# Context squares kept out of PSUM, the residual's gate row moved beside the heads of x, and another share of PSUM for the output units

## The chip, the cores and the metric

The kernel runs on one core of one Trainium2 chip. The metric is the device time of one execution in microseconds (us). TensorE is the engine PE of the profile, VectorE is DVE, ScalarE is ACT, GpSimd is POOL, SyncE is SP; SP computes nothing here and issues most DMAs.

## What is computed

One layer of a hybrid backbone on 1024 latent tokens (`x`) and 256 context tokens (`ctx`), width 2048, all in fp32. Cut to what matters:

```
mod = silu(c) @ w_mod + b_mod           # shift, scale and gate rows; ctx uses c_ctx
h   = rmsnorm(x) * (1 + scale) + shift  # the same for ctx with its own row
q,k,v,o,z,gates,xr,zr = split(h @ w_in) # x and ctx share the weights
A = mlstm(q, k, v, gates) * sigmoid(o) * silu(z)       # 4 heads, both directions, state from ctx
B = rglru(conv(xr)) * silu(zr)                         # 8 tiles of 128 channels, both directions
out = rmsnorm(x + gate * (concat(A, B) @ w_out)) * final_g
```

The change concerns the norm of ctx (the mean of its squares over 2048 channels), the row `gate` of `mod` (2048 numbers), the softplus of the RG-LRU's `lambda`, and the accumulators of the last matmul.

## The kernel before

Every fp32 product is made of three fp32r products: a weight tile `raw` comes by DMA on SP (`Ring._dma`, L206), ACT rounds it to `whi` (L227), DVE takes the rest `wlo = raw - whi` (L228), and PE multiplies hi by hi, hi by lo and lo by hi. The class `Ring` does this ahead of use, with two or three pieces in hand.

The work runs in five stages. **Phase A** (to about 169 us of the span) squares x, multiplies the modulation weights `wm` with silu(c) and silu(c_ctx) (`mv_group`, L471), turns x into normalised tiles `hxh`/`hxl` (`to_hx`, L536 to L542), and beside that accumulates the first three column tiles of `h @ w_in` (`main_a`, L595). In it the context norm is computed: at the end of iterations j = 2 and 3, `ctx_norms` squares four pairs of ctx tiles in one go (L559) into PSUM tiles `mx`, and DVE adds them up (L561, L563); `ctx_pair` then makes `hch`/`hcl` (L577 to L581), one tile k after the other through a single buffer `ft`. The order on PE, DVE, ACT and SP in phase A is the order of the code (`in_order`). **The context heads** (to about 360 us) begin with V of ctx (`cv`, L976 to L978); ahead of it stand the evacuation of phase A's three accumulators (L659 to L669) and the softplus chain of lambda (L674 on). **The heads of x** (to about 1167 us) interleave column tiles (L1200 to L1206), V (L1243 to L1246) and the mLSTM scans (`scan_gen`, L1131 on; its decay rows `NI` come by DMA on SP, L1079). The context's RG-LRU, `ctx_rg_all`, runs beside them in slots `RS` of 128x260. **The rg stage** (to about 1533 us) computes column tiles xr and zr and, beside them, the RG-LRU of x (`rg_gen`: L689 conv, L904 to L906 scan, L920; L1308 to L1320 gates), and also the residual's gate row (`gt_gen`, L1329 to L1350): 64 weight tiles `gw` of 128x512 come by DMA through two buffers, DVE multiplies and adds each into `ga` (L1336, L1338), four matmuls with ones sum over the partitions (L1344), and a DMA stores the row. **The output units** (to the end) multiply with `w_out` (L1425 to L1427), eight units of 512 tokens by 512 columns.

After phase A the order comes from a planner: `Clock` holds the side work as generators, each of which yields an estimated time, and takes the next step of each when the main work's `tick` has advanced that far. PSUM has two tiles `mm` of two banks and four tiles `mx` of one bank. An output unit needs four banks:

```
if db % 2:
    return [mx_tile() for _ in range(4)]
two = [mm_tile() for _ in range(2)]
```

A `ct_unit` of the rg stage also uses `mm`, and L1407/L1408 evacuate it.

Of the kernel before, what the change touches and what calls it, by code (L numbers as in the profile page):

```python
# [150 lines left out]
class Ring:  # L151


    def __init__(self, tc, pool, nraw, npc, raw_el, pc_el):
# [10 lines left out]
        self.pri = 0  # L165

# [47 lines left out]
    def _split(self):  # L214
# [33 lines left out]
def tile_hymba(ctx: ExitStack, tc: tile.TileContext, x, x_t, ctx_t, vecs_t, w_mod_a, w_mod_g, b_mod, w_in,  # L248
# [182 lines left out]
    def load_ctx(j):  # L431
        for k in (2 * j, 2 * j + 1):
            Xc[k] = hcs.tile([128, CTX], F32, tag="cl", bufs=KT, name=f"cT{k}")
            SP.dma_start(out=Xc[k], in_=ctx_t[k])

    def phase_a():
        ACT.dma_start(out=cols, in_=vecs_t[:, 0:216])
        cc = pa.tile([128, 4, 16], F32, tag="ft", bufs=1, name="cc")
# [15 lines left out]
        del cc  # L454
        DVE.tensor_scalar(out=b1sc, in0=cols[:, cSC:cSC + 16], scalar1=1.0, scalar2=None, op0=ADD)
# [99 lines left out]
        def ctx_norms(js):  # L555
# [43 lines left out]
        ctx_at = {4: (0, 1), 5: (2, 3), 6: (4, 5), 7: (6, 7)}  # L599
        for j in range(KP):  # L600
            for u in range(2):
# [972 lines left out]
```

## Time and profile before

| | us |
|---|---|
| median of 3 runs (1921.99 to 1927.17) | 1925.8 |
| the profiled execution | 1922.13 |
| its span, first to last instruction | 1920.4 |
| PE busy | 1825.2 (95%) |
| DVE busy | 891.8 (46%) |
| ACT busy | 778.4 (41%) |
| POOL busy | 280.9 (15%) |

The mean granted clock of TensorE was 0.982 of full speed. Busy shares are means over stages; where PE waited must be read stage by stage. In a timeline row the bracket at the end tells how long the engine had been idle before the row and what ended it. In a row of windows the number behind each engine is its busy time and, in parentheses, how many instructions.

### The profile page before, as it was taken

How to read it: one execution, taken by the hardware profiler on the slowest of the kernel's cores; microseconds unless marked ns; L12 is line 12 of the kernel's file. 1: busy time of each engine (PE TensorE's matmuls, PEld its weight loads, DVE VectorE, ACT ScalarE, POOL GpSimd, SP SyncE). 2: the span in 40 equal slices, each digit the busy share in tenths (PEclk: the TensorE clock that was granted, in tenths of full speed). 3: DMA queues.
4: the chain of work that ended last, by engine and by line, in shares of the span. 5: the costliest groups of instructions: out<-in, count | busy, mean ns of one | idle time of the engine just before them, and what ended most of it. 6: DMA issues, size and time to landing. Idle time of an engine off the chain costs nothing.

```text
span 1920.4 us, 23817 instructions
## 1 busy us (share of the span) xinstructions
PE 1825.2 (95%) x9106; PEld 1489.9 (78%) x9106; DVE 891.8 (46%) x1565; ACT 778.4 (41%) x1214; POOL 280.9 (15%) x382
## 2 busy tenths in 40 slices
PE   7888999999999999999999999889899989999997
PEld 2446999888897879887898878667777767887786
DVE  5556653445434542145213435775575555334432
ACT  5335543336735531133113334455555554224322
POOL 0000001012101110011001201221212323222221
PEclk9999999999999999999999999899999989999999
DMA  9965575213222222122121215333342336446533
GB/s 382 337 212 169 166 195 142 78 50 69 64 72 56 52 65 66 45 55 68 55 60 45 66 34 154 109 110 96 89 131 70 105 119 200 129 132 220 167 113 132
DMA packets 217283, 224.48 MB, mean 117 GB/s; under 512 B 24760, under 2 KB 169272, under 8 KB 217168
## 3 DMA queue, kind: packets, MB, share of 16 engines
q1 hardware_dynamic: 209128, 199.16, 35.0%
q10 hardware_dynamic: 5256, 14.88, 2.1%
q0 software_dynamic: 2784, 8.92, 1.4%
q8 instruction: 71, 1.16, 0.2%
q14 instruction: 44, 0.36, 0.1%
HBM read 202.92 MB, written 20.00 MB: 116 GB/s over the span
## 4 chain that ended last, share of the span: by engine, by line
PE 74%; DMA 9%; DVE 8%; issue 4%; ACT 3%; POOL 1%; ACTq 0%; SPq 0%; DVEq 0%; POOLq 0%
PE mm L1206 12%; PE mm L1200 12%; PE mm L1203 12%; PE mm L595 2%; PE mm L1243 2%; PE mm L1245 2%; PE mm L1246 2%; DMA gw<-in_w_mod_g_dram 2%; DMA yst<-yD 2%; PE mx L1426 2%; PE mx L1427 2%; PE mx L1425 2%; PE mm L1425 2%; PE mm L1426 2%; PE mm L1427 2%
## 5 line engine op out<-in xcount | busy, mean ns | idle before, releaser
L228 DVE TENSOR_TENSOR wlo<-raw,whi 128x512 fp32r<-128x512 f32 (+2 forms) x396 | 285.8, 731 | 599.3 <-ACT whi L227 598.4
L227 ACT ACTIVATE whi<-raw 128x512 fp32r<-128x512 f32 (+2 forms) x396 | 243.4, 624 | 603.1 <-PE mm L1203 254.0
L1206 PE MATMUL mm<-hxh,wlo 128*128 128x512 f32 x1184 | 377.2, 400 | 14.2 <-DVE wlo L228 14.1
L1200 PE MATMUL mm<-hxh,whi 128*128 128x512 f32 x1184 | 388.3, 409 | 0.3 <-DVE Gx L1232 0.3
L1203 PE MATMUL mm<-hxl,whi 128*128 128x512 f32 x1184 | 374.4, 397 | 0.0
L1206 PEld LDWEIGHTS mm<-hxh,wlo 128*128 128x128 f32 x1184 | 224.9, 190 | 67.8 <-DVE wlo L228 16.4
L1203 PEld LDWEIGHTS mm<-hxl,whi 128*128 128x128 f32 x1184 | 224.6, 190 | 53.0
L1200 PEld LDWEIGHTS mm<-hxh,whi 128*128 128x128 f32 x1184 | 222.9, 190 | 50.7 <-issue 1.4
L1243 PE MATMUL mm<-whi,hxh 128*128 128x256 f32 x384 | 109.9, 286 | 0.4 <-DVE s L1281 0.2
L1425 PE MATMUL mm<-whi,hxh 128*128 128x512 f32 x256 | 102.7, 402 | 6.4 <-DVE s L1408 6.2
L1245 PE MATMUL mm<-wlo,hxh 128*128 128x256 f32 x384 | 108.2, 282 | 0.0
L1246 PE MATMUL mm<-whi,hxl 128*128 128x256 f32 x384 | 107.6, 281 | 0.0
L1426 PE MATMUL mm<-wlo,hxh 128*128 128x512 f32 x256 | 102.7, 401 | 2.7 <-DVE wlo L228 2.7
L1427 PE MATMUL mm<-whi,hxl 128*128 128x512 f32 x256 | 102.1, 399 | 0.0
L1425 PE MATMUL mx<-whi,hxh 128*128 128x512 f32 x192 | 76.1, 397 | 4.0 <-ACT whi L227 4.0
L1426 PE MATMUL mx<-wlo,hxh 128*128 128x512 f32 x192 | 76.0, 396 | 1.7 <-DVE wlo L228 1.7
L1427 PE MATMUL mx<-whi,hxl 128*128 128x512 f32 x192 | 75.5, 393 | 0.0
L1338 DVE SCALAR_TENSOR_TENSOR ga<-gw,cols,ga 128x512 f32<-128x512 f32 x60 | 55.1, 918 | 43.7 <-DMA gw<-in_w_mod_g_dram 43.2
L1243 PEld LDWEIGHTS mm<-whi,hxh 128*128 128x128 f32 x384 | 72.6, 189 | 1.2 <-issue 0.5
L1245 PEld LDWEIGHTS mm<-wlo,hxh 128*128 128x128 f32 x384 | 72.5, 189 | 0.3
L1246 PEld LDWEIGHTS mm<-whi,hxl 128*128 128x128 f32 x384 | 72.3, 189 | 0.0
L1103 ACT ACTIVATE D<-D,gxAC 128x128 f32<-128x128 f32 x64 | 25.4, 401 | 107.6 <-POOL D L1102 107.4
(320 smaller groups left out, 3092.5 us busy)
## 6 DMA issues: line engine op xcount, KB each, us to landing
raw<-in_w_in_dram SPq DMA_DIRECT2D x134, 512.0 KB, 4.0
wm<-in_w_mod_a_dram SPq DMA_DIRECT2D x64, 512.0 KB, 8.8
raw<-in_w_out_dram SPq DMA_DIRECT2D x64, 512.0 KB, 4.7
gw<-in_w_mod_g_dram SPq DMA_DIRECT2D x64, 256.0 KB, 3.1
xT<-in_x_t_dram SPq DMA_DIRECT2D x16, 512.0 KB, 8.9
NI<-niD SPq DMA_DIRECT2D x64, 128.0 KB, 4.6
xpc<-in_x_dram SPq DMA_DIRECT2D x32, 256.0 KB, 3.4
yD<-s ACTq DMA_DIRECT2D x15, 512.0 KB, 2.9
```

Of the source, the lines that this page charges most:

```text
L227: self.nc.scalar.activation(out=hi, in_=src, func=AF.Copy)
L228: self.nc.vector.tensor_tensor(out=lo, in0=src, in1=hi.bitcast(F32), op=SUB)
L1200: PE.matmul(out=ps[:, ts], lhsT=hi, rhs=hxh[k][:, ts], start=(k == 0), stop=False)
L1203: PE.matmul(out=ps[:, ts], lhsT=hi, rhs=hxl[k][:, ts], start=False, stop=False)
L1206: PE.matmul(out=ps[:, ts], lhsT=lo, rhs=hxh[k][:, ts], start=False, stop=(k == KT - 1))
L1243: PE.matmul(out=o, lhsT=hxh[k][:, sl], rhs=hi, start=(k == 0 and tt % 2 == 0), stop=False, skip_group_check=True)
L1245: PE.matmul(out=o, lhsT=hxh[k][:, sl], rhs=lo, start=False, stop=False, skip_group_check=True)
L1246: PE.matmul(out=o, lhsT=hxl[k][:, sl], rhs=hi, start=False, stop=(k == KT - 1), skip_group_check=True)
L1338: DVE.scalar_tensor_tensor(out=a, in0=t, scalar=silc[:, k:k + 1], in1=a, op0=MUL, op1=ADD)
L1425: PE.matmul(out=pst[jt], lhsT=hxh[j][:, sl], rhs=hi, start=(j == 0), stop=False)
L1426: PE.matmul(out=pst[jt], lhsT=hxh[j][:, sl], rhs=lo, start=False, stop=False)
L1427: PE.matmul(out=pst[jt], lhsT=hxl[j][:, sl], rhs=hi, start=False, stop=(j == KT - 1))
```

## The change

It has seven parts. (1) ctx is loaded in 8 tiles of two k each, and `ctx_norm(j)` squares one such tile in one 512-wide instruction into a half of the SBUF tile `ncp`, one behind each group of modulation matmuls in iterations 2 and 3. (2) `ctx_pair` takes both k of a pair through two halves of `vt`. (3) `Ring` holds back the raw loads of phase A to the beginning of the next iteration. (4) The softplus chain of lambda moves to the beginning of phase A. (5) The first V of ctx is written inside phase A's ordered block, and the evacuation of the accumulators is spread over its k. (6) `gt_gen` goes; `gate_row` follows the context's RG-LRU as a tail of `ctx_rg_all`, in slots `RS`, with 128 tiles of 128x256 and three in flight. (7) Each output unit takes one `mm` tile and two `mx` tiles.

```
+    def release(self):
+        while self.held:
+            self.held -= 1
             self._dma()
...
-            for j in js:
-                sq = mx_tile()
-                for u in range(2):
-                    act(out=sq[:, CTX * u:CTX * u + CTX], in_=Xc[2 * j + u], func=AF.Square)
-                if j == 0:
-                    DVE.tensor_copy(out=ncp[0][:, 0:512], in_=sq)
-                else:
-                    DVE.tensor_tensor(out=ncp[0][:, 0:512], in0=ncp[0][:, 0:512], in1=sq, op=ADD)
+        def ctx_norm(j):
+            sq, sm = ncp[0][:, 512:1024], ncp[0][:, 0:512]
+            act(out=sq if j else sm, in_=Xc[j].rearrange("p u t -> p (u t)"), func=AF.Square)
+            if j:
+                DVE.tensor_tensor(out=sm, in0=sm, in1=sq, op=ADD)
...
+                        if j in (2, 3):
+                            ctx_norm(4 * j - 8 + g)
...
-            if j in (2, 3):
-                ctx_norms(range(4 * j - 8, 4 * j - 4))
...
+        def put_away(k):
+            if k == 4:
+                gate_tile(0)
+            elif k == 6:
+                gate_tile(1)
+            elif k == 8:
+                raw_tile(2, 2)
+        raw_tile(0, 0)
+        ps_v = cv_products(0, put_away)
...
-        xflag["rgctx"] = True
+        yield from gate_row(RS)
+    def gate_row(RS):
+        W = 256
+        todo = [(db, k) for db in range(D // W) for k in range(KT)]
...
+            t = yield from RS.get()
+            SP.dma_start(out=t[:, 0:W], in_=wmod_k[:, k, db * W:(db + 1) * W])
...
+                DVE.scalar_tensor_tensor(out=a, in0=t, scalar=silc[:, k:k + 1], in1=a, op0=MUL, op1=ADD)
+            RS.free()
+            if n + 3 < len(todo):
+                yield from load(n + 3)
+            yield 2.7
+            if k == KT - 1:
+                ps = mx_tile()
+                PE.matmul(out=ps[:, 0:W], lhsT=ones, rhs=a, start=True, stop=True)
...
-    clk.spawn(gt_gen(), 1.0, P['gt'])
...
     def out_tiles(db):
-        if db % 2:
-            return [mx_tile() for _ in range(4)]
-        two = [mm_tile() for _ in range(2)]
-        return [two[j // 2][:, 512 * (j % 2):512 * (j % 2) + 512] for j in range(4)]
+        two = mm_tile()
+        return [two[:, 0:512], two[:, 512:1024], mx_tile(), mx_tile()]
```

How the instructions stand on an engine before and now, at three places. In a row a number behind a name tells buffers of one name apart.

ACT in phase A, iteration 2, before: the squares stand in one block behind the four `hxh`.

```order
L478 ACTIVATE pmS_631<-mx_577 128x512
L537 ACTIVATE hxh_646<-rxt,ssa 128x512 x2
L537 ACTIVATE hxh_654<-rxt,ssa 128x512 x2
L559 ACTIVATE mx_676<-cT_356 128x256
L559 ACTIVATE mx_676<-cT_358 128x256
L559 ACTIVATE mx_680<-cT_360 128x256
L559 ACTIVATE mx_680<-cT_362 128x256
L559 ACTIVATE mx_684<-cT_364 128x256
L559 ACTIVATE mx_684<-cT_366 128x256
L559 ACTIVATE mx_688<-cT_368 128x256
L559 ACTIVATE mx_688<-cT_370 128x256
L227 ACTIVATE whi_692<-raw_517 128x384
```

The same iteration now:

```order
L228 ACTIVATE whi_577<-raw_471 128x384
L591 ACTIVATE ncp<-cT_376 128x512
L591 ACTIVATE ncp<-cT_378 128x512
L591 ACTIVATE ncp<-cT_380 128x512
L228 ACTIVATE whi_625<-raw_471 128x384
L512 ACTIVATE pmS_637<-mx_581 128x512
L591 ACTIVATE ncp<-cT_382 128x512
L571 ACTIVATE hxh_654<-rxt,ssa 128x512 x2
L571 ACTIVATE hxh_662<-rxt,ssa 128x512 x2
L228 ACTIVATE whi_687<-raw_574 128x384
```

Eight squares of one k became four of two k, they write SBUF, and they stand ahead of `hxh`. The line numbers of the changed kernel are its own: its L228, L512, L571 and L591 are L227, L478, L537 and L559 of before.

DVE in the rg stage, around the two scans of one tile, before (L1338 is the gate row, L904 to L906 the scan):

```order
L228 TENSOR_TENSOR wlo_10986<-raw_10703,whi_10985 128x512
L1338 SCALAR_TENSOR_TENSOR ga_10969<-gw_7_11134,cols,ga_10969 128x512
L1338 SCALAR_TENSOR_TENSOR ga_10969<-gw_8_11161,cols,ga_10969 128x512
L904 SCALAR_TENSOR_TENSOR s_10856<-s_10979,s_10856 128x1024
L904 SCALAR_TENSOR_TENSOR s_10911<-s_10982,s_10911 128x1024
L905 TENSOR_TENSOR s_10856<-s_10856,s_10887 128x1024
L905 TENSOR_TENSOR s_10911<-s_10911,s_10943 128x1024
L906 SCALAR_TENSOR_TENSOR s_10887<-s_10979,rini,s_10856 128x1024
L906 SCALAR_TENSOR_TENSOR s_10943<-s_10982,rini,s_10911 128x1024
L228 TENSOR_TENSOR wlo_11030<-raw_10795,whi_11029 128x512
```

And now, where L957 to L959 are that scan:

```order
L229 TENSOR_TENSOR wlo_10967<-raw_10737,whi_10966 128x512
L957 SCALAR_TENSOR_TENSOR s_10847<-s_10960,s_10847 128x1024
L957 SCALAR_TENSOR_TENSOR s_10901<-s_10963,s_10901 128x1024
L958 TENSOR_TENSOR s_10847<-s_10847,s_10877 128x1024
L958 TENSOR_TENSOR s_10901<-s_10901,s_10930 128x1024
L959 SCALAR_TENSOR_TENSOR s_10877<-s_10960,rini,s_10847 128x1024
L959 SCALAR_TENSOR_TENSOR s_10930<-s_10963,rini,s_10901 128x1024
L229 TENSOR_TENSOR wlo_11003<-raw_10737,whi_11002 128x512
```

Nothing stands between the weight split and the scan any more.

DVE beside the scan of head 1 in the heads of x, as it is now (L1033 is the gate row, L1215 to L1222 belong to the mLSTM scan); before, the same scan rows (L1142, L1144, L1139, L1146) followed the split directly:

```order
L1033 SCALAR_TENSOR_TENSOR r_5743<-r_6031,cols,r_5743 128x256
L229 TENSOR_TENSOR wlo_5900<-raw_5561,whi_5899 128x512
L1033 SCALAR_TENSOR_TENSOR r_5743<-r_6066,cols,r_5743 128x256
L1033 SCALAR_TENSOR_TENSOR r_5743<-r_6119,cols,r_5743 128x256
L1033 SCALAR_TENSOR_TENSOR r_5743<-r_6159,cols,r_5743 128x256
L1033 SCALAR_TENSOR_TENSOR r_5743<-r_6202,cols,r_5743 128x256
L1218 TENSOR_SCALAR dn_1_0_5924<-mx_5917,EM 128x1
L1220 TENSOR_SCALAR dn_1_0_5924<-mx_5917,dn_1_0_5924 128x1
L1215 SCALAR_TENSOR_TENSOR C_1_0_5922<-C_0_0_5834,NI_1_0_5776,mx_5920 128x257
L1222 RECIPROCAL dn_1_0_5924<-dn_1_0_5924 128x1
L1218 TENSOR_SCALAR dn_1_1_5936<-mx_5929,EM 128x1
L1033 SCALAR_TENSOR_TENSOR r_5743<-r_6242,cols,r_5743 128x256
```

Six multiply-adds of the gate row came in among the rows of one chunk.

SP in the same place, before:

```order
L206 DMA raw_5690<-in_w_in_dram 128x8x128
L1079 DMA NI_2_0_5898<-niD 128x2x128
L1079 DMA NI_2_1_5900<-niD 128x2x128
L206 DMA raw_5786<-in_w_in_dram 128x8x128
L1079 DMA NI_3_0_5980<-niD 128x2x128
L1079 DMA NI_3_1_5982<-niD 128x2x128
L1079 DMA NI_4_0_6063<-niD 128x2x128
L1079 DMA NI_4_1_6065<-niD 128x2x128
L206 DMA raw_5936<-in_w_in_dram 128x8x128
```

And now (L1017 loads a weight tile of the gate row, L1155 a decay row, L207 a weight tile of the main work):

```order
L1155 DMA NI_2_0_5862<-niD 128x2x128
L1017 DMA r_6066<-in_w_mod_g_dram 128x256
L1155 DMA NI_2_1_5864<-niD 128x2x128
L1017 DMA r_6119<-in_w_mod_g_dram 128x256
L1017 DMA r_6159<-in_w_mod_g_dram 128x256
L1017 DMA r_6202<-in_w_mod_g_dram 128x256
L207 DMA raw_5735<-in_w_in_dram 128x8x128
L1017 DMA r_6242<-in_w_mod_g_dram 128x256
L1017 DMA r_6287<-in_w_mod_g_dram 128x256
L1017 DMA r_6327<-in_w_mod_g_dram 128x256
L1017 DMA r_6354<-in_w_mod_g_dram 128x256
L1155 DMA NI_3_0_5950<-niD 128x2x128
```

The loads of NI and raw stand behind loads of the gate row, each of which waits for a free slot.

## Rows read from the trace of the kernel before

**Rows 1.** The page: busy time of the engines, and the chain by engine.

```profile
PE 1825.2 (95%) x9106; PEld 1489.9 (78%) x9106; DVE 891.8 (46%) x1565; ACT 778.4 (41%) x1214; POOL 280.9 (15%) x382
...
PE 74%; DMA 9%; DVE 8%; issue 4%; ACT 3%; POOL 1%; ACTq 0%; SPq 0%; DVEq 0%; POOLq 0%
```

**Rows 2.** Windows of the rg stage: length, busy of five engines (count), PEclk, DMA, GB/s.

```profile
1200.00:1220.00 20.00, 13.24 (x50) 10.36 (x49) 17.32 (x16) 4.43 (x7) 0.84 (x1) 0.79 0.30 85
1240.00:1260.00 20.00, 16.91 (x74) 13.40 (x73) 17.69 (x17) 7.10 (x8) 3.31 (x1) 1.00 0.22 59
1280.00:1300.00 20.00, 14.13 (x50) 11.00 (x50) 17.43 (x14) 4.76 (x6) 4.48 (x2) 0.83 0.33 89
1300.00:1320.00 20.00, 16.58 (x63) 12.44 (x62) 7.95 (x10) 8.52 (x11) 2.41 (x1) 0.91 0.27 79
1320.00:1340.00 20.00, 20.00 (x88) 16.19 (x87) 11.29 (x12) 16.15 (x17) 2.49 (x3) 1.00 0.42 113
1340.00:1360.00 20.00, 14.83 (x55) 11.63 (x54) 17.29 (x17) 3.75 (x4) 6.04 (x2) 0.83 0.38 115
```

**Rows 3.** Timeline of phase A, PE: start, us, instruction, idle before.

```profile
91.95 1.93 PE L471 MATMUL mx<-wm,silP 128*32 128x512 f32 x8 [5.71 <-issue]
98.66 1.07 PE L471 MATMUL mx<-wm,silP 128*32 128x512 f32 x8
112.81 1.94 PE L471 MATMUL mx<-wm,silP 128*32 128x512 f32 x8 [5.72 <-issue]
```

**Rows 4.** Timeline of phase A, ACT and DVE.

```profile
88.76 3.14 ACT L559 ACTIVATE mx<-cT 128x256 f32<-128x256 f32 x8
...
90.37 2.27 DVE L563 TENSOR_TENSOR ncp<-ncp,mx 128x512 f32<-128x512 f32 x3
```

**Rows 5.** Windows of phase A, columns as in rows 2.

```profile
40.00:60.00 20.00, 19.84 (x100) 10.02 (x100) 12.38 (x23) 7.40 (x12) 0.00 (x0) 1.00 1.03 396
80.00:100.00 20.00, 14.29 (x70) 7.33 (x70) 9.91 (x19) 7.23 (x15) 0.00 (x0) 0.83 0.74 272
100.00:120.00 20.00, 14.28 (x68) 8.21 (x66) 11.66 (x21) 7.70 (x16) 0.00 (x0) 0.91 0.53 183
```

**Rows 6.** Timeline at the end of phase A, PE and ACT.

```profile
174.47 0.59 PE L976 MATMUL mm<-whi,hch 128*128 128x272 f32 x1 [3.56 <-ACT whi L227]
...
181.34 1.21 ACT L227 ACTIVATE whi<-raw 128x544 fp32r<-128x544 f32 x2 [4.03 <-DMA raw<-in_w_in_dram]
```

**Rows 7.** The page: the gate row's group on DVE, with mean ns and idle.

```profile
L1338 DVE SCALAR_TENSOR_TENSOR ga<-gw,cols,ga 128x512 f32<-128x512 f32 x60 | 55.1, 918 | 43.7 <-DMA gw<-in_w_mod_g_dram 43.2
```

**Rows 8.** The chain between 1320 and 1352 us: start, us, what.

```profile
1334.81 4.03 DMA gw<-in_w_mod_g_dram
1338.92 0.76 DVE ga L1338
...
1350.15 1.22 PE mm L1206 x2
```

**Rows 9.** Waits of PE between 1200 and 1360 us: total, times, longest.

```profile
PE mm L1206 <- DVE wlo L228: 14.1, 3, 5.9
PE mx L1318 <- ACT s L1312: 9.6, 2, 6.8
```

**Rows 10.** Timeline at the first output unit, PE and DVE, and the window behind.

```profile
1539.79 0.76 PE L1425 MATMUL mm<-whi,hxh 128*128 128x512 f32 x1 [6.25 <-DVE s L1408]
...
1537.65 1.99 DVE L1408 TENSOR_TENSOR s<-mm,s 128x1024 f32<-128x1024 f32 x1 [1.10 <-ACT s L1407]
...
1540.00:1560.00 20.00, 18.10 (x64) 13.85 (x65) 8.83 (x11) 14.04 (x17) 3.48 (x3) 0.84 0.17 54
```

**Rows 11.** A multiply-add of half the width, and the loads of both sizes.

```profile
L577 DVE SCALAR_TENSOR_TENSOR ft<-cT,ssa,rcB 128x256 f32<-128x256 f32 x16 | 7.7, 484 | 0.5
...
gw<-in_w_mod_g_dram SPq DMA_DIRECT2D x64, 256.0 KB, 3.1
...
NI<-niD SPq DMA_DIRECT2D x64, 128.0 KB, 4.6
```

**Rows 12.** The heads of x: two windows, a wait of PE, a link of the chain.

```profile
640.00:680.00 40.00, 40.00 (x189) 33.45 (x188) 18.79 (x69) 16.41 (x30) 8.98 (x20) 1.00 0.25 55
680.00:720.00 40.00, 38.28 (x168) 31.02 (x168) 18.22 (x55) 14.65 (x33) 4.40 (x9) 1.00 0.27 71
...
PE mx L1110 <- DVE C L1139: 4.3, 3, 1.6
...
685.58 4.38 DMA NI<-niD
```

More of the change, by code (lines that the diff above doesn't have):

```diff
@@ L650, in jv, with cv_products @@
         return ap.rearrange("p (w r) -> p w r", r=GR)
+    def cv_products(h, hook=None):
+        ps = mm_tile()
+        w = 272 if h == 0 else 256
+        for k, hi, lo in pieces(("cv", h)):
+            for tt in range(NCC):
+                o = ps[:, 512 * tt:512 * tt + w]
+                sl = slice(tt * 128, (tt + 1) * 128)
+                PE.matmul(out=o, lhsT=hch[:, k, sl], rhs=hi, start=(k == 0), stop=False)
+                PE.matmul(out=o, lhsT=hch[:, k, sl], rhs=lo, start=False, stop=False)
+                PE.matmul(out=o, lhsT=hcl[k][:, sl], rhs=hi, start=False, stop=(k == KT - 1))
+            clk.tick(6 * T256)
+            if hook:
+                hook(k)
+        return ps
@@ L652, in tile_hymba, with pieces @@
+    def pieces(key):
+        k = 0
+        for p in pcs[key]:
+            hi, lo = ring.get(p)
+            for j in range(ring.pieces[p][2]):
+                yield k, hi[:, j, :], lo[:, j, :]
+                k += 1
     with in_order(tc, PE.engine, DVE.engine, ACT.engine, SP.engine):
         acc = phase_a()
-    st = [pa.tile([128, SEQ], F32, tag="wm", bufs=NWM, name=f"stx{i}") for i in range(2)]
-    stz = pa.tile([128, 2, SEQ], F32, tag="xp", bufs=1, name="stz")
-    for hf in range(2):
-        ws = slice(32 * hf, 32 * hf + 32)
-        act(out=j2r(st[0])[:, ws, :], in_=jv(acc[0][hf]), func=AF.Copy)
@@ L680, in tile_hymba, with raw_tile @@
-    DVE.tensor_scalar(out=negS, in0=hafS, scalar1=-8.0, scalar2=None, op0=MUL)
-    DVE.tensor_scalar(out=hafS, in0=hafS, scalar1=4.0, scalar2=None, op0=MUL)
+        halves = [slice(32 * hf, 32 * hf + 32) for hf in range(2)]
+        def raw_tile(n, m):
+            st = pa.tile([128, SEQ], F32, tag="wm", bufs=NWM, name=f"stx{n}")
+            for hf in range(2):
+                act(out=j2r(st)[:, halves[hf], :], in_=jv(acc[m][hf]), func=AF.Copy)
+            acc[m] = None
+            ACT.dma_start(out=pre[n], in_=st)
@@ new lines, in gate_tile @@
+        def gate_tile(hf):
+            if hf == 0:
+                acc.append(pa.tile([128, 2, SEQ], F32, tag="xp", bufs=1, name="stz"))
+            stz = acc[3]
+            sg = stz[:, 0, 512 * hf:512 * hf + 512]
+            act(out=sg, in_=acc[1][hf], func=AF.Sigmoid)
+            DVE.tensor_tensor(out=j2r(stz[:, 1, :])[:, halves[hf], :], in0=jv(acc[1][hf]), in1=jv(sg), op=MUL)
+            if hf:
+                ACT.dma_start(out=pre[1], in_=stz[:, 1, :])
+                acc[1] = None
@@ L952, in ctx_rg_all, with load @@
             yield 2.0
-        xflag["rgctx"] = True
+        yield from gate_row(RS)
+    def gate_row(RS):
+        W = 256
+        todo = [(db, k) for db in range(D // W) for k in range(KT)]
+        tiles = []
+        def load(n):
+            db, k = todo[n]
+            t = yield from RS.get()
+            SP.dma_start(out=t[:, 0:W], in_=wmod_k[:, k, db * W:(db + 1) * W])
+            tiles.append(t)
+        for n in range(3):
+            yield from load(n)
+        yield 3.0
+        for n, (db, k) in enumerate(todo):
+            if k == 0:
+                a = yield from RS.get()
+                a = a[:, 0:W]
+                br = yield from RS.get()
+                SP.dma_start(out=br[0:1, 0:W], in_=b_mod[:, 2 * D + db * W:2 * D + (db + 1) * W])
+            t = tiles.pop(0)[:, 0:W]
+            if k == 0:
+                DVE.tensor_scalar(out=a, in0=t, scalar1=silc[:, 0:1], scalar2=None, op0=MUL)
+            else:
+                DVE.scalar_tensor_tensor(out=a, in0=t, scalar=silc[:, k:k + 1], in1=a, op0=MUL, op1=ADD)
[6 more added lines that the diff above has]
+                PE.matmul(out=ps[:, 0:W], lhsT=ones, rhs=a, start=True, stop=True)
+                clk.pe(4 * T256)
+                yield 2.0
+                DVE.tensor_tensor(out=br[0:1, 0:W], in0=ps[0:1, 0:W], in1=br[0:1, 0:W], op=ADD)
+                yield 1.0
+                ACT.dma_start(out=gtD[:, db * W:(db + 1) * W], in_=br[0:1, 0:W])
+                RS.free(2)
     def prods(o, kt, k, kstart, kend, hi, lo, act_h, act_l, first=True):
```

128 lines of the change are left out of this document (47 added, 81 removed).

## The prediction, made before the changed kernel ran

> **What bounds the kernel now.** I read the page first: PE is busy 95% of the span and carries 74% of the chain [rows 1]; no other engine is near half of that in the chain. So the time is PE's work plus PE's holes, and the change adds no matmul columns worth a term (eight gate matmuls of half width for four, nine V matmuls merely moved). Then I cut the span into windows of 20 us and counted PE's matmuls. A window of the rg stage without a hole holds 88 of them [rows 2], 20/88 = 0.227 us each; a window with n has lost (88 - n) x 0.227 us, idle time and half-speed clock together. The granted clock is at 0.79 to 0.83 in the windows where PE had stood for over 5 us, and at 1.00 in the window 1240 to 1260 whose hole was about 3 us [rows 2], so a long hole costs twice: once as idle, once as the stretch at the 1.2 GHz level behind it.
>
> Holes lie in four places, and the timelines say what ends each: in phase A behind the ctx squares [rows 3, 4], at the end of phase A [rows 6], in the rg stage behind the DVE [rows 8, 9], and at the first output unit [rows 10].
>
> **Squares of ctx.** PE stands 5.71 and 5.72 us ahead of the modulation matmuls of the next iteration [rows 3]. "Issue" hides the cause; the rows of the other engines tell it: in that gap ACT runs the eight squares and DVE adds them up [rows 4], and both use the rotating `mx` tiles, of which phase A's third accumulator holds two, so the modulation accumulator waits for a tile. Behind the hole eight matmuls take 1.93 us against 1.07 undisturbed [rows 3], and about two such groups' worth of work runs slow, some 1.8 us. So each hole costs 5.7 + 1.8 = 7.5 us, two 15 us. The changed order has four 512-wide squares per iteration, in SBUF, ahead of `hxh`: no PSUM tile is wanted, and no lump. Could the weights then be late? DMA is full between 40 and 60 us (396 GB/s) but at 272 and 183 GB/s in the two windows with the holes [rows 5], so there is room. I take 12 of the 15 us; the ends are 3 (squares now delay `hxh`, or the `wm` loads become the wait) and 15.
>
> **Context pairs, lambda, held raw loads.** Two steps on each engine now overlap where one waited for the other; PE's one hole behind them was below 2 us. I take 1 us, between 0 and 2. The lambda chain at the start is 17 operations of 16 elements and one table load, beside the arrival of the x tiles, which that part waits for anyway: nothing; without that cover some 4 us.
>
> **End of phase A.** The first split of V's second weight piece stands on ACT behind the evacuation of six accumulator halves and a table load; PE waits 3.56 us, then runs at half clock, and the next raw piece comes 4.03 us late [rows 6]. With the clock this is about 7 us. The spread evacuation puts the splits first. But V then asks for raw tiles faster than two buffers gave them here, so I take 4, between 0 and 7.
>
> **Gate row out of the rg stage.** Its 60 multiply-adds are busy 55.1 us and wait another 43.2 us for their DMAs [rows 7]. DVE executes in order, so a scan that is ready stands behind a multiply-add that waits for its tile, and the weight split `wlo` behind the scan. The chain shows it: tile `gw` lands, `ga`, then the scan, then `wlo`, then PE at 1350.15 [rows 8]. The waits are the 14.1 us on `wlo` and the 9.6 us behind the RG-LRU's gate input [rows 9]. By matmul counts the five windows lose 38, 14, 38, 25 and 33 matmuls [rows 2], that is 8.6, 3.2, 8.6, 5.7 and 7.5 us, together 33.6. What stays: the two scans themselves (two each of L904, L905, L906) still stand ahead of `wlo`, and in the first window the conv and the gate input do too, with or without a gate row. I keep 5.6 of the first window, all of the second, 2.1 of the third, 1.2 and 1.5 of the last two, 13.6 in all: 20 us come back. Ends: 8 (the scans alone hold `wlo` as long in three of the windows) and 27.
>
> **Output units.** The first unit needs both `mm` tiles, and the second of them is only free when L1408 has evacuated the last zr tile: PE stands 6.25 us, and the window behind runs at 0.84 with 64 matmuls, (88 - 64) x 0.227 = 5.5 us lost [rows 10]; together 11.8. With one `mm` and two `mx` the unit starts while that tile is evacuated. About 1.8 us of it is a later wait on `wlo`, and something of the evacuation remains, so 8 come back, between 5 and 11.
>
> **Gate row into the heads of x.** DVE gets 120 multiply-adds and 8 products of half the width: the nearest row is 0.484 us [rows 11], 128 x 0.484 = 62 us, over a stretch of some 500 us in which DVE is busy 18.8 of 40 us in its fullest windows [rows 12]. That alone is hidden. Loads: the trace gives 3.1 us for a 256 KB tile and 4.6 us for a 128 KB one [rows 11]; with three in flight 128 of them need 128 x 3.1/3 = 132 to 128 x 4.6/3 = 196 us of those 500, hidden too. The Trainium skill (Perfetto Trace Analysis, DMA Optimizations) speaks against this cut: it says transfers of under 2 KB carry a significant overhead each and advises fewer and larger ones, while the new rows are 1 KB where the old were 2 KB. NI, the slower row here, also has 1 KB per partition, so the trace agrees in its direction; by the page the slower rival below would gain weight.
>
> What is not hidden is the order. SP issues in order, and two loads of NI of head 1 now stand behind gate loads that wait for a slot, that is for a multiply-add; on DVE six of these stand among the scan rows of one chunk. NI was on the chain already (4.38 us at 685.58), and PE lost 4.3 us to the state `C` in three heads [rows 12]. Heads 1 and 2 get some 40 tiles inside their scans. I charge one late NI and one late multiply-add, 1.5 us each, to either head: 6 us. Ends: 0, as three loads in flight cover the latency, and 15, when every second one of the 16 in the fullest chunks waits 1.5 us and the clock drops once.
>
> **Sum.** 12 + 1 + 4 + 20 + 8 = 45 saved, 6 paid: 39 us. From the profiled execution's 1922.1 this gives 1883.1; the median of the runs is 3.7 higher, 1925.8, which gives 1886.8. I say **1885**.
>
> **Rivals.** *The scans hold the rg stage.* DVE's own chain (two scans, conv, gate input), not the gate row, sets `wlo`, since in the first windows all of it stands in one row. For it: DVE is busy 17.3 of 20 us in the holes [rows 2]. Against: 43.2 us of the gate row's time there are waits for DMAs [rows 7]. Then 8 instead of 20 come back: about 1897. Chance 0.17.
>
> *Phase A turns to its loads.* With the holes gone, PE asks for `wm` and raw sooner; DMA is full until 60 us [rows 5]. Then 3 + 0 instead of 12 + 4: 1898. Chance 0.12.
>
> *The gate row stalls the scans* (the other side). SP's and DVE's orders lock: a gate load waits for a multiply-add, NI and raw wait behind the load, the scan waits for NI, and the next multiply-add stands behind the scan. For it: rows of SP and DVE as they now stand, and the link of NI in the chain [rows 12]. Against: DMA share is 0.25 there and three tiles are in flight. Its price: 40 tiles inside scans x 1.5 us (4.6/3) = 60 us instead of 6, against 45 saved: 1937. It decides from 45/40 = 1.1 us of PE per tile on. Chance 0.09.
>
> *Output and rg together stay*, because other rows take the place of the gate row's (the part doesn't do what it says): 8 and 5 come back instead of 20 and 8: 1900. Chance 0.04.
>
> **Numbers.** Forecast 0.58, rivals as above. The low end takes good ends of several parts at once (rg 27, phase A 15, its end 6, output 11, heads 2: 19 us more): 1866. The high end takes the first two rivals together (12 + 13 on top of 1885) and some of the heads' 15: 1914. That leaves the slower rival and the extremes out. A measurement of this kernel can tell 0.3%, 5.8 us, from no change. Slower: the third rival, 0.08; same: its mild half and the worst ends together, 0.05; faster 0.87.
>
> **What would show it.** Right: no hole over 3 us behind the squares and 88 matmuls per 20 us soon after; no wait over 2 us ahead of L976; windows of the rg stage at 80 and more where no two scans stand; the first output unit's wait below 2 us; in the heads, windows of head 1 and 2 not more than 3 us below before. Wrong: waits of scan rows on multiply-adds of the gate row or NI landing late by several us per chunk, PE waits on `wlo` as long as before with no gate row ahead, or a new wait on `wm`.

## The result, and the profile after

The change takes 1893.05 us (median of 4 runs, 1890.24 to 1898.41) against 1923.89 (4 runs beside it, 1921.85 to 1927.17): ratio 0.984, 95% interval 0.981 to 0.987. The interval lies below 1, so the change is faster, by 1.6%; the time is 8 us above the forecast of 1885 and inside its range of 1866 to 1914. The profiled execution took 1890.24 us, its span 1888.5 against 1920.4; the mean granted clock rose from 0.982 to 0.990.

The page of the change, engines and chain, against [rows 1]:

```profile
PE 1815.2 (96%) x9114; PEld 1483.5 (79%) x9114; DVE 896.5 (47%) x1632; ACT 779.7 (41%) x1209; POOL 284.5 (15%) x382
...
PE 61%; DMA 12%; issue 11%; DVE 7%; ACT 6%; POOL 3%; SPq 0%; ACTq 0%; POOLq 0%; DVEq 0%
```

PE is still the bound. To see where the 32 us come from, I set the start of each PE instruction before against that of the same one after; the difference, the **offset**, grows where the change gains and falls where it pays.

| place | offset at its end, us | change, us | forecast, us |
|---|---|---|---|
| phase A and its end | 22.1 | +22.1 | +17 (12 + 1 + 4) |
| heads of x | 15.6 | -6.5 | -6 |
| rg stage | 39.4 | +23.8 | +20 |
| output units up to the last | 40.1 | +0.7 | +8 (first unit) |
| last output unit | 31.9 | -8.2 | none |

Of the heads' loss, 3.4 us are the eight gate matmuls, which moved there from the rg stage; so the rg stage itself gave 20.4, and 3.1 us of the loss are waits and the clock behind them. Not all of these are the gate row's: see h1_no_loads and h2_no_mults below.

**Phase A.** Timeline of PE: the two holes of [rows 3] are gone, and of [rows 6] a third is left. What remains of some length is a wait for modulation weights and one for the evacuation:

```profile
119.10 1.05 PE L505 MATMUL mx<-wm,silP 128*32 128x512 f32 x4 [0.83 <-DMA wm<-in_w_mod_a_dram]
...
150.74 0.39 PE L686 MATMUL mm<-whi,hch 128*128 128x272 f32 x1 [1.24 <-ACT stx L709]
```

What ended the two holes can be read in the kernel before. Phase A's third accumulator holds two of the four `mx` tiles, so the squares take turns in the other two, and the modulation accumulator behind them gets the tile of the third square. In both iterations DVE's third operation on the squares, which frees that tile, ends 0.10 us ahead of PE's start at 91.95 and 112.81 [rows 3]:

```profile
91.16 0.69 DVE L563 TENSOR_TENSOR ncp<-ncp,mx 128x512 f32<-128x512 f32 x1
...
112.02 0.69 DVE L563 TENSOR_TENSOR ncp<-ncp,mx 128x512 f32<-128x512 f32 x1
```

A third wait of before, behind the second hole, belongs to the context pairs: ACT makes `pmS` behind the last `hch`, and PE's transposes wait for it. After the change it is gone.

```profile
125.26 0.51 ACT L579 ACTIVATE hch<-ft,ssa 128x256 fp32r<-128x256 f32 x1 [1.07 <-DVE ft L577]
...
126.09 0.57 ACT L478 ACTIVATE pmS<-mx 128x512 f32<-128x512 f32 x1
126.72 0.66 PE L486 MATMUL mx<-ident,pmS 128*128 128x128 f32 x4 [1.77 <-ACT pmS L478]
```

**Heads of x.** Waits of PE on the state `C` between 560 and 1160 us (total, times, longest): 7.2 us, where [rows 12] had 4.3.

```profile
PE mx L1186 <- DVE C L1215: 5.2, 3, 2.1
PE mx L1185 <- DVE C L1215: 2.0, 2, 1.7
```

**The rg stage.** The same view between 1160 and 1320 us, against [rows 9]: 23.7 us have become 9.3.

```profile
PE mx L1394 <- ACT s L1388: 5.1, 3, 3.3
PE mm L1282 <- DVE wlo L229: 4.2, 2, 3.3
```

Its windows, against [rows 2]: five lost 14 to 38 matmuls; now every second one here is full, and the worst, at 1220, lacks 26: there a scan (L959) and the next tile's conv (L742) stand ahead of `wlo` on DVE, with no gate row near (last three rows, of DVE).

```profile
1220.00:1240.00 20.00, 16.70 (x62) 13.09 (x61) 17.27 (x15) 9.06 (x11) 3.29 (x1) 0.83 0.13 33
1240.00:1260.00 20.00, 20.00 (x88) 16.20 (x87) 6.44 (x7) 17.32 (x20) 4.88 (x4) 1.00 0.17 54
1260.00:1280.00 20.00, 17.46 (x74) 13.31 (x73) 18.73 (x14) 6.62 (x7) 7.24 (x2) 1.00 0.30 85
1280.00:1300.00 20.00, 20.00 (x88) 16.16 (x87) 3.51 (x3) 14.34 (x16) 4.49 (x2) 1.00 0.11 27
...
1226.85 2.35 DVE L959 TENSOR_TENSOR_SCAN s<-s,rini,s 128x1024 f32<-128x1024 f32 x1
1229.11 1.26 DVE L742 SCALAR_TENSOR_TENSOR s<-s,cols,s 128x1024 f32<-128x1024 f32 x1
1230.29 0.68 DVE L229 TENSOR_TENSOR wlo<-raw,whi 128x512 fp32r<-128x512 f32 x1
```

**First output unit.** The 6.25 us of [rows 10] are gone: the unit starts 46.3 us earlier than before. Then PE waits again, now for the unit's own weights, and the 6 us are given back (timeline of ACT and PE, and the window; L952 is RG-LRU work of the last tile):

```profile
1513.21 2.19 ACT L952 ACTIVATE s<-s,tiny 128x1024 f32<-128x1024 f32 x2
1515.31 1.66 ACT L228 ACTIVATE whi<-raw 128x512 fp32r<-128x512 f32 x3
1515.97 0.50 PE L1475 MATMUL mm<-whi,hxh 128*128 128x512 f32 x1 [2.52 <-ACT whi L228]
1518.55 0.79 PE L1476 MATMUL mm<-wlo,hxh 128*128 128x512 f32 x1 [1.41 <-DVE wlo L229]
...
1500.00:1520.00 20.00, 15.28 (x55) 11.09 (x54) 11.55 (x12) 16.84 (x20) 3.50 (x3) 0.84 0.16 54
```

**Last output unit**, PE, ACT and DVE, in order of time. Here stands a wait that was not there before:

```profile
1838.04 0.69 DVE L1512 TENSOR_TENSOR res<-mm,gt 128x512 f32<-128x512 f32 x1 [8.75 <-PE mm L1565]
1844.73 0.69 DVE L1513 TENSOR_TENSOR res<-res,xpc 128x512 f32<-128x512 f32 x1 [5.99 <-DMA xpc<-in_x_dram]
1845.45 0.60 ACT L1514 ACTIVATE mm<-res 128x512 f32<-128x512 f32 x1 [3.18 <-DVE res L1513]
1846.23 0.79 PE L1563 MATMUL mm<-hxh 128*128 128x512 f32 x1 [5.73 <-ACT mm L1514]
...
1840.00:1860.00 20.00, 14.27 (x54) 11.26 (x53) 2.69 (x6) 2.89 (x6) 2.52 (x2) 0.83 0.29 93
```

The last unit runs token tile by token tile. Its first two accumulators are now halves of one `mm` tile. The first is done at 1838.0. Its evacuation waits 5.99 us for a piece of x, and its step L1514 writes the square back into that half. PE takes twelve matmuls of the third tile ahead, until 1840.5, and then stands; its matmul into the other half starts 0.2 us behind L1514. Before, this unit had four separate `mx` tiles, and its windows were full (88 to 90 matmuls):

```profile
1870.00:1890.00 20.00, 20.00 (x90) 16.55 (x89) 4.68 (x9) 4.34 (x10) 7.79 (x7) 1.00 0.31 86
```

### The profile page after: what moved, and what is told of

It reads as the page before. It is cut to its first block, busy times and chain, and to the rows that moved or that the text cites. A ratio compares the mean times of both kernels' runs of the same rounds, so it can differ in the third digit from the quotient of the medians.

```text
span 1888.5 us, 24095 instructions
## 1 busy us (share of the span) xinstructions
PE 1815.2 (96%) x9114; PEld 1483.5 (79%) x9114; DVE 896.5 (47%) x1632; ACT 779.7 (41%) x1209; POOL 284.5 (15%) x382
## 4 chain that ended last, share of the span: by engine, by line
PE 61%; DMA 12%; issue 11%; DVE 7%; ACT 6%; POOL 3%; SPq 0%; ACTq 0%; POOLq 0%; DVEq 0%
PE mm L1282 11%; PE mm L1276 11%; PE mm L1279 11%; DMA xpc<-in_x_dram 5%; PE mm L1319 2%; PE mm L1321 2%; PE mm L1322 2%; DMA yst<-yD 2%; POOL res L1513 2%; PE mm L627 2%; PE mx L505 1%; DMA r<-in_w_mod_g_dram 1%; PE mx L1207 1%; DMA wm<-in_w_mod_a_dram 1%; PE mx L1208 1%
## 5 line engine op out<-in xcount | busy, mean ns | idle before, releaser
L228 ACT ACTIVATE whi<-raw 128x512 fp32r<-128x512 f32 (+2 forms) x396 | 243.2, 624 | 561.5 <-PE mm L1279 247.2
L1475 PE MATMUL mm<-whi,hxh 128*128 128x512 f32 x224 | 90.1, 402 | 6.3 <-ACT whi L228 6.1
L1476 PE MATMUL mm<-wlo,hxh 128*128 128x512 f32 x224 | 90.4, 404 | 3.3 <-DVE wlo L229 3.3
L1477 PE MATMUL mm<-whi,hxl 128*128 128x512 f32 x224 | 89.4, 399 | 0.0
L1476 PE MATMUL mx<-wlo,hxh 128*128 128x512 f32 x224 | 89.0, 397 | 0.0
L1475 PE MATMUL mx<-whi,hxh 128*128 128x512 f32 x224 | 89.0, 400 | 0.0
L1477 PE MATMUL mx<-whi,hxl 128*128 128x512 f32 x224 | 88.8, 396 | 0.0
L1033 DVE SCALAR_TENSOR_TENSOR r<-r,cols,r 128x256 f32<-128x256 f32 x120 | 60.5, 504 | 38.0 <-DMA r<-in_w_mod_g_dram 35.9
```

Source lines behind the costliest of these rows:

```text
L228: self.nc.scalar.activation(out=hi, in_=src, func=AF.Copy)
L1033: DVE.scalar_tensor_tensor(out=a, in0=t, scalar=silc[:, k:k + 1], in1=a, op0=MUL, op1=ADD)
L1475: PE.matmul(out=pst[jt], lhsT=hxh[j][:, sl], rhs=hi, start=(j == 0), stop=False)
L1476: PE.matmul(out=pst[jt], lhsT=hxh[j][:, sl], rhs=lo, start=False, stop=False)
L1477: PE.matmul(out=pst[jt], lhsT=hxl[j][:, sl], rhs=hi, start=False, stop=(j == KT - 1))
```

## The experiments

Theory: the gains come from the places the prediction names, and the 8 us that are missing are the shared tile in the last unit. Rivals: the output units' part is worth nothing anywhere; the row's loads, or its multiply-adds, cost the heads more than they show; the squares' lump, not their PSUM tiles, made the holes. The kernel before measured 1923.9 to 1931.1 in the five groups of runs, so ratios to the kernel before of the same group are given beside the times, and small differences are read from offsets in the trace. The change itself was run in the first group alone (1923.9) and t1_tail_order in the second alone (1927.4). A difference between runs of two groups is therefore uncertain by several us, and offsets between their traces can hold such a difference too.

### t1_tail_order: the last unit's tiles in another order

```
     pst = out_tiles(3)
+    pst = [pst[0], pst[2], pst[3], pst[1]]
```

> The last output unit takes its four accumulators in the order first half of mm, mx, mx, second half of mm. If PE stood 5.73 us near the end because the second token tile's accumulator shared a tile with the first one, which was still being evacuated, the hole and the slow clock behind it go: about 8 us less than the changed kernel, 1885. If the evacuation itself (loads of x and of the two rows, DVE, ACT) holds the tail, the hole only moves to another tile: 1893, the same as the changed kernel.

Measured: 1885.81 us (1884.64 to 1890.17), 0.978 [0.976, 0.980]. Window of the last unit:

```profile
1840.00:1860.00 20.00, 20.00 (x90) 16.54 (x89) 6.13 (x12) 5.26 (x12) 3.88 (x3) 1.00 0.54 172
```

The hole is gone and with it 7 us by the medians, 8.2 by the offset in the last unit. This version beats both kernels; most later experiments start from it.

### t2_old_tiles: the old sharing of PSUM

```
-        two = mm_tile()
-        return [two[:, 0:512], two[:, 512:1024], mx_tile(), mx_tile()]
+        if db % 2:
+            return [mx_tile() for _ in range(4)]
+        two = [mm_tile() for _ in range(2)]
+        return [two[j // 2][:, 512 * (j % 2):512 * (j % 2) + 512] for j in range(4)]
```

> The changed kernel with the sharing of PSUM by output units as it was before (two mm or four mx). If the new sharing gained nothing in the end at the first unit (its 7 us of head start were eaten by the waits for y and for weight splits within three units) and cost 8 us in the tail, this is about 7 us faster than the changed kernel: 1886. If the first unit's start is worth what the prediction said, 8 us are lost there and 8 won in the tail: 1893.

Measured: 1887.12 us (1883.77 to 1889.11), 0.978 [0.976, 0.980]. Timeline of PE: the old wait for the evacuation is back,

```profile
1504.40 0.77 PE L1477 MATMUL mm<-whi,hxh 128*128 128x512 f32 x1 [6.68 <-DVE s L1460]
```

and the last unit has no hole. So the new sharing gained nothing that lasts at the first unit and lost 6 us by the medians (8.2 by offset) at the last: this part, forecast at +8, was worth -6 to -7.5. Against t1_tail_order, in the same group, the old sharing is no slower (1887.12 and 1885.81).

### o1_yb4: four buffers for the finished rows

```
-YB, K0, K1 = 2, 4, 10
+YB, K0, K1 = 4, 4, 10
```

> Base: t1_tail_order, 1885.8 us. One number: 4 buffers instead of 2 for the loads of the finished y rows that are split for the first output units. If the 8 us of waits in the first output unit come from ScalarE standing in its order at a split of y whose load could only start when one of two buffers was free, they shrink by half or more and the offset at the first output unit, which fell from 46.3 to 40 us, keeps 3 to 5 us of it: 1881 to 1883 us. If ScalarE is late there because of the last tile's RG-LRU work that stands ahead of the weight splits, more buffers change nothing: 1886 (1884 to 1888).

Measured: 1886.31 us (1886.26 to 1889.18), 0.978 [0.976, 0.980]: no different from t1_tail_order. The offsets of the two profiles say more. Between 1486 and 1547 us o1_yb4 gains 3.8 us, as the first theory has it; but it had come to 1486 us 5.9 us late, of which some 3 arose before 420 us and some 3 between 1120 and 1365 us, in stretches that don't use these buffers. So by its trace the buffers do hold ScalarE there, but by the time nothing is gained, and why it was late ahead of them is open.

### g1_gate_back: the gate row in the rg stage again

```
-        yield from gate_row(RS)
+        xflag["rgctx"] = True
...
+    clk.spawn(gt_gen(), 1.0, P['gt'])
```

> The changed kernel with the gate row back in the rg stage, as 64 tiles of 128x512. If the gate row's multiply-adds held scans and weight splits there, the rg stage loses about 24 us and the heads of x win about 6.5: 1893 + 17 = 1910. If the rg stage had come down for another reason (its work starts in another phase of the loads now, or the scans hold it either way), the time stays near 1893 or falls by the 6.5 us.

Measured: 1913.40 us (1910.27 to 1915.15), 0.992 [0.990, 0.993], 20 us above the change. Waits of PE between 1160 and 1400 us:

```profile
PE mm L1282 <- DVE wlo L229: 13.1, 3, 5.2
PE mx L1394 <- ACT s L1388: 10.0, 3, 6.4
```

These are the waits of [rows 9]. By offset against t1_tail_order, from the same group, the heads give back 3.8 us (3.4 of them the moved matmuls) and the rg stage loses 25; the time is 28 us above t1_tail_order, 8 of them the last unit's hole. The rival that the scans alone hold `wlo` falls.

### h1_no_loads and h2_no_mults: what the row costs the heads

Two halves of the row, both on t1_tail_order. h1_no_loads keeps the multiply-adds and leaves out 125 of the 128 weight loads; h2_no_mults keeps the loads and leaves out the 120 multiply-adds.

```
 # h1
-            t = tiles.pop(0)[:, 0:W]
+            t = keep[n % 3][:, 0:W]
...
-            RS.free()
-            if n + 3 < len(todo):
-                yield from load(n + 3)
```

```
 # h2
-            else:
-                DVE.scalar_tensor_tensor(out=a, in0=t, scalar=silc[:, k:k + 1], in1=a, op0=MUL, op1=ADD)
```

> On top of the other order in the tail (t1_tail_order, 1885.8). The gate row's multiply-adds stay in their places, but all read the first three weight tiles, which are loaded once: 125 of the 128 loads are left out, so the gate row is computed from too few weights. If SP's queue (NI and raw behind gate loads) and the multiply-adds' waits for DMA cost the heads of x their additional idle time, some 4 us come back: 1882, and the scan's waits on C fall to those of the kernel before (1.42, 1.20, 1.64). If what the heads lost is the eight gate matmuls (about 3.4 us of PE work that only moved) and DVE's own load, it stays at 1886.

> On top of t1_tail_order. All 128 loads stay, but 120 multiply-adds are left out (each gate block is only its first product). If the multiply-adds among the scan rows hold the scans (DVE in order), some 4 us come back: 1882. If the loads on SP's queue do it, it stays at 1886 while the waits on C stay as long as in the changed kernel (2.11, 1.75 and 1.35, 1.70).

Measured: h1_no_loads 1883.04 us (1880.40 to 1885.19), 0.976 [0.974, 0.978]; h2_no_mults 1898.47 (1895.68 to 1901.10), 0.984 [0.982, 0.985]. Leaving the multiply-adds out made the kernel *slower*, by 12 us in the medians and 10 in the heads by offset. The largest wait on the state `C` in the heads, h1_no_loads first, then h2_no_mults (t1_tail_order: 8.1 us in all):

```profile
PE mx L1185 <- DVE C L1214: 5.4, 3, 2.1
```

```profile
PE mx L1184 <- DVE C L1213: 12.6, 5, 4.1
```

Timeline of SP in h2_no_mults. A row is the issuing of a DMA, its wait for a free slot included:

```profile
637.88 0.38 SPq L1153 DMA_DIRECT2D NI<-niD  x1
640.37 6.59 SPq L1017 DMA_DIRECT2D r<-in_w_mod_g_dram  x6
647.06 0.38 SPq L1153 DMA_DIRECT2D NI<-niD  x1
```

Six loads of the row hold SP for 6.59 us, and the next decay row `NI` of the scan stands behind them. So the order on SP's queue can cost the heads some 10 us; the multiply-adds on DVE cost nothing that shows.

What the row costs there as the change places it is much less. g1_gate_back and a4_phase_a_only (below) have no gate row in the heads at all, and PE's waits on `C` are still above the 4.3 us of the kernel before, 6.2 and 4.7 (g1_gate_back first):

```profile
PE mx L1186 <- DVE C L1215: 6.2, 3, 2.5
...
PE mx L1186 <- DVE C L1215: 4.7, 3, 1.8
```

With the row they are 6.1 to 8.1 us over seven versions whose heads are the same program (t1_tail_order has the longest), and without its loads or without them inside the scans 5.4. So the loads cost some 1 to 2 us of waiting, little more than these versions spread. The offset against the kernel before falls in the heads of these two by 5.7 and 3.7 us too, where the change lost 6.5 and t1_tail_order, with the same heads, 9.6. Hence a gain of 3 us in the heads is no more than these versions differ among themselves, and the 2.8 us that h1_no_loads ends ahead of t1_tail_order there by offset don't show more. What else makes the heads lose is open.

### b2_gate_skips_scan: the row stands still while a scan is issued

```
+            while "busy" in xflag:
+                yield 0.5
             t = tiles.pop(0)[:, 0:W]
```

(`scan_gen` sets the flag ahead of its loop and takes it away behind it.)

> Base: the change with the last unit's tiles in the other order (t1_tail_order, 1885.8 us). The gate row's loop waits while a head's mLSTM scan is being issued, so that no load of the row (SP's queue) and no multiply-add stands between the loads of the scan's rows; the row is done before the RG-LRU stage all the same. If it is the row's loads on SP's queue that hold back the scans' own loads, TensorE's waits on the states C in the heads of x fall from 8.1 us towards the 4.3 us of the kernel before: about 1882 us (1880 to 1884). If the scans are late for another reason (ScalarE, GpSimd, their own length), the waits stay near 8 and the time stays at 1886 (1884 to 1888). If the row moved out of the scans holds up the steps between them (q and k of the next head), new waits of 3 us or more come before a scan and it ends at 1889 or above.

Measured: 1901.76 us (1898.33 to 1902.92), 0.986 [0.984, 0.988]: slower than t1_tail_order by some 15. Waits in the heads, and in the rg stage:

```profile
PE mx L1189 <- DVE C L1218: 5.4, 3, 2.1
...
PE mm L1286 <- DVE wlo L229: 6.7, 2, 5.7
PE mx L1398 <- ACT s L1392: 6.5, 2, 5.5
PE mx L1042 <- DVE r L1035: 2.2, 1, 2.2
```

In the heads it goes the way the theory says: the waits fall from 8.1 to 5.4 us and the offset against t1_tail_order rises from -0.6 at 600 us to +5.0 at 1090. But the row's last sums now come at 1140 and 1161 us (L1042 waits 2.2 us), inside the rg stage, whose waits rise to 17.3 us from 9.9. None of the three expectations named this; the third had the size and not the place.

### c1_skip_fast_ctx16: the pause with a faster pace, and ctx in 16 loads

```
-            yield 2.7
+            yield 1.8
...
-        SP.dma_start(out=Xc[j], in_=ctx_t[j])
+        for u in range(2):
+            SP.dma_start(out=Xc[j][:, u, :], in_=ctx_t[j][:, u, :])
```

> Base: t1_tail_order (1885.8 us); two edits in stages that don't meet, read apart by the offset of TensorE's instructions against t1_tail_order. (1) As in b2_gate_skips_scan the gate row stands still while a scan of the heads is issued, but its pace outside them goes from 2.7 to 1.8, so that its last sum comes on TensorE before the heads of x end. b2_gate_skips_scan gained 5.0 us in the heads and lost more than 15 behind them. If that loss came from the row's reaching into the RG-LRU stage, the gain of 4 to 5 us in the heads now stays to the end; if the loss came from something else that the pause moves, the offset falls below zero again behind 1100 us; if the faster pace itself holds up the weight splits on VectorE, the gain of the heads is missing. (2) ctx is loaded by 16 DMAs of 128 KB again, as before the change, in place of 8. If the longer time of those loads on SP's queue made the 3.6 us by which the kernel before is late ahead of its first squares, the offset is -3 to -4 us at 80 us with new waits on the modulation weights at 65 to 80 us; else it is 0 there. Times: 1882 if only the first holds, 1885 if both, 1889 if only the second, 1897 or more if the loss behind the heads returns.

Measured: 1885.96 us (1885.51 to 1892.92), 0.978 [0.975, 0.980], near the 1885 expected if both hold. The offset against t1_tail_order is -3.9 us at 83 us and -4.1 at 420; it comes back to -1.3 in the heads and is -1.3 at the end. Timeline of PE, the new waits:

```profile
69.38 2.14 PE L506 MATMUL mx<-wm,silP 128*32 128x512 f32 x8 [1.66 <-DMA wm<-in_w_mod_a_dram]
...
78.33 1.05 PE L506 MATMUL mx<-wm,silP 128*32 128x512 f32 x4 [1.43 <-DMA wm<-in_w_mod_a_dram]
...
52.21 11.72 SPq L444 DMA_DIRECT2D cT<-in_ctx_t_dram  x16
```

The last row is SP's: 16 loads of ctx hold its queue for 11.72 us (11.97 in the kernel before); the change's eight loads of the same bytes take

```profile
52.33 7.93 SPq L443 DMA_DIRECT2D cT<-in_ctx_t_dram  x8
```

and the weights behind them are issued some 4 us sooner. The Trainium skill (Perfetto Trace Analysis, DMA Optimizations) advises to batch small transfers into larger ones; here the trace agrees, 11.72 us for 16 loads with rows of 1 KB against 7.93 us for eight with rows of 2 KB; whether the number of loads or the length of the rows makes it isn't shown. For the gate row the same page would have spoken against the change, and there the size of the rows did not decide. Once the row ends within the heads, the loss of b2_gate_skips_scan behind them is gone, which speaks for the row's reaching into the rg stage as its cause. The 2.8 us that the pause gains in the heads are kept to the end, but the change, without a pause, gains 3.1 us on t1_tail_order in the same stretch; so the pause isn't shown to gain. The pause with eight ctx loads wasn't run.

### a1_psum_spread, a5_lump_sbuf: two corners of the squares

a1_psum_spread starts from the change and puts each square into an `mx` tile, spread as in the change. a5_lump_sbuf starts from t1_tail_order and keeps the squares in SBUF, but four in a row behind the split of x.

```
 # a1
-            sq, sm = ncp[0][:, 512:1024], ncp[0][:, 0:512]
-            act(out=sq if j else sm, in_=Xc[j].rearrange("p u t -> p (u t)"), func=AF.Square)
+            sq, sm = mx_tile(), ncp[0][:, 0:512]
+            act(out=sq, in_=Xc[j].rearrange("p u t -> p (u t)"), func=AF.Square)
...
```

```
 # a5
-                        if j in (2, 3):
-                            ctx_norm(4 * j - 8 + g)
...
-                    if j in (2, 3):
-                        ctx_norm(4 * j - 5)
...
+            if j in (2, 3):
+                for q in range(4 * j - 8, 4 * j - 4):
+                    ctx_norm(q)
```

> The changed kernel with the squares of ctx written into PSUM tiles again, but still spread, one behind each group of modulation matmuls. If the claim on a PSUM tile made the two holes of 5.7 us, PE waits for tiles again in iterations 2 and 3, eight times by about 1.5 us or more, 10 us and more in all: 1903. If the lump of eight squares behind hxh made them, spreading alone is enough: 1893.

> Base: t1_tail_order, 1885.8 us. The squares of ctx stay in SBUF, but the four of an iteration stand in one lump behind its split of x, as in the kernel before. Together with a1_psum_spread (in PSUM, but spread: no hole in phase A) this makes the four corners. If the lump alone makes the holes of the kernel before, both come back and it ends 8 to 17 us later: 1894 to 1903. If the lump hurts only because its squares stand in PSUM tiles that TensorE's sums wait for, there is no hole at the end of those two iterations and it stays at 1886 (1884 to 1888). In between (the lump holds back only what stands behind it on ScalarE and VectorE): 1888 to 1893.

Measured: a1_psum_spread 1898.40 us (1891.45 to 1902.98), 0.983 [0.981, 0.986]; a5_lump_sbuf 1892.57 (1890.41 to 1897.50), 0.981 [0.979, 0.983]. a1_psum_spread has no hole at the squares; PE is 1.5 us later than in the change at 150 us and 3.6 at 200. The rest of its difference lies in stages that the edit doesn't touch and is open; by its ratio it equals the change. a5_lump_sbuf has one hole, behind the second lump (PE and DVE):

```profile
103.98 0.69 DVE L593 TENSOR_TENSOR ncp<-ncp 128x512 f32<-128x512 f32 x1 [0.70 <-ACT ncp L591]
104.82 2.05 PE L598 MATMUL mx<-ncp,ones 128*128 128x256 f32 x4 [5.73 <-DVE ncp L593]
```

With the clock behind it, it costs 8.8 us by offset. It isn't the second hole of before come back. There PE stood at the modulation matmuls (L471); in a5_lump_sbuf these run on time, and up to the sum the offset against the kernel before is 17.7 us, as in t1_tail_order (17.8). What waits now is the matmul that sums the squares (L598): it stands just behind the lump's four squares and four sums, which take each other's turn on ACT and DVE, 1.4 us a pair. Before, PE came to that sum late, because of the hole ahead of it, and did not wait there. So both holes of before need both, the lump and its PSUM tiles: either one alone makes none of them. But the lump in SBUF opens a new one at the sum, so the squares had to be spread as well.

### a2_no_hold and a4_phase_a_only: the rest of phase A, and phase A alone

a2_no_hold (on t1_tail_order) lets the raw loads of phase A go at once; a4_phase_a_only keeps the phase A parts of the change alone, with the gate row and the tiles as before (the edits of g1_gate_back and t2_old_tiles together).

```
 # a2
-        ring.held = 0
+        ring.held = None
...
-            ring.release()
-            if j == KP - 1:
-                ring.held = None
```

> On top of t1_tail_order, with the raw loads of phase A issued at once again instead of held behind the modulation weights. Phase A had gained 3.6 us before the first hole, where the prediction charged nothing. If the held loads made that (the waits of 0.5 to 1.1 us on wm between 68 and 76 us come back), this is 3 to 4 us slower: 1889. If the eight larger loads of ctx made it, the time stays at 1886.

> The changed kernel with the gate row back in the rg stage and the old sharing of PSUM: only the parts in phase A and at its end are left. If the parts add up as the traces say (22 us gained by the first V of ctx and kept), this is 1926 - 22 = 1904. If the gain in phase A is given back later (the loads or the scans of the heads take it up), it lies above 1912.

Measured: a2_no_hold 1887.60 us (1885.02 to 1891.78), 0.978 [0.977, 0.980]: the held loads are worth nothing that shows. a4_phase_a_only 1906.15 us (1903.26 to 1909.10), 0.988 [0.986, 0.989], that is 24 us below the kernel before beside it (1930.26). By the times, what phase A gives (22 us) reaches the end whole. Its trace against the one of the kernel before ends 13.5 us ahead, but that trace comes from the first group, in which the kernel before is 6.4 us faster, and a4_phase_a_only was profiled in its slowest run.

The pairing of the context tiles and the place of the lambda chain were not run alone.

## Why the prediction was right, and where it failed

**What bounds the kernel** held: PE, and the four places of its holes. A gain in phase A came out at the end in full by the times (a4_phase_a_only).

**Squares of ctx** (12, between 3 and 15): right in place and in reason. Around the two holes the offset grew from 3.6 to 10.9 and from there to 18.1 us, 7.3 and 7.1, against the 7.5 that the prediction worked out for each; the discount from 15 to 12 was not needed. The reason, a missing `mx` tile, holds for both holes (a1_psum_spread and a5_lump_sbuf: neither the tiles nor the lump alone makes them). That the squares also had to be spread, because of the sum behind them, it did not say.

**Context pairs, lambda, held loads** (1, between 0 and 2): the wait behind the pairs (1.77 us) went and gave 1.9; the hold gave nothing. With the lambda chain ahead of it PE's first matmul starts 3.5 us later (13.02 against 9.49), and by 33 us that is made up, as forecast. Outside this list, the eight ctx loads gave 3.6 to 3.9 us ahead of the first hole (c1_skip_fast_ctx16). The prediction gave this edit no price, though the waits on `wm` between 68 and 76 us stood in the trace of before (0.51, 0.82 and 1.06 us).

**End of phase A** (4, between 0 and 7): 2.1, as PE still waits for the evacuation (1.24 us), then three times for `whi` by 0.5 to 0.8 us, and 1.41 for DVE's `c`.

**Gate row out of the rg stage** (20): 23.8 by offset, 20.4 without the moved matmuls. The waits on `wlo` and on the gate input fell by the 14.4 us that the views show; the rest, some 6 us, is put down to the slower clock behind these waits (granted 0.79 to 0.91 in four windows of [rows 2], 0.83 in one here). g1_gate_back brings the waits back.

**Gate row into the heads** (-6): -6.5, and that it agrees in size is luck. 3.4 of it are the moved matmuls, which the prediction left out as no term, and of the other 3.1 a part is lost, by their traces, without the row too (g1_gate_back, a4_phase_a_only). It named two prices, a late `NI` and a late multiply-add, 6 us together. Of the second nothing shows; of the first 1 to 2 us of waiting on `C`. The rival in which the row stalls the scans has its mechanism on the chip, in h2_no_mults, at some 10 us and not at its 54.

**The step that failed** is "8 come back" of the output units. Its mechanism was right (the unit starts while the last zr tile is evacuated), its consequence was not followed to the next late thing: PE, earlier, waits for `whi`, which ScalarE makes in its order behind the splits of the finished rows and the last tile's RG-LRU work (`whi` at 1515.31 behind L952). And the same edit was not costed at the other units: in the last one two token tiles now share an `mm` tile, 8.2 us. Together -7.5 instead of +8; the other terms came to 39.4 instead of 31, 3.6 of it from the ctx loads that had no term. The two errors partly cancel, and that much of the forecast's nearness is luck: the one by itself would have put the forecast 8 us too high, the other 15 too low.

## What to carry to other kernels

A change in how accumulators share PSUM is to be costed at every unit that draws on it, above all at the last, where a matmul may wait for the evacuation of the other half of its tile; the order of use alone (t1_tail_order) gave 7 us. Background work is to be placed by the queue that it shares, and not only by the share of its engine: ask which load stands behind the one that waits for a slot (h2_no_mults). A lump may hide a second wait behind the one that it makes (a5_lump_sbuf). And a small loss is the change's only if it is missing in a version without it (g1_gate_back). When a start is pulled ahead, read what is late next before the gain is booked.

## What was not expected of the hardware

Of the same 2 MB of ctx, 16 loads held SP's queue 11.7 to 12.0 us and eight 7.9. And 120 multiply-adds fewer on DVE made the kernel 10 to 12 us slower; its trace shows the loads that had waited for them in bunches (6.59 us for six) ahead of the scan's own.
